# Experts' weights in 2 MB transfers, paired attention heads and a shorter one-hot path in a two-block forward pass

## The chip, the cores and the metric

The kernel runs on one core of a Trainium2 chip. A core has the matmul engine TensorE (PE in the profile, its weight loads are PEld), the element-wise engines VectorE (DVE), ScalarE (ACT) and GpSimd (POOL), SyncE (SP), which here issues nearly all of the large transfers, and 16 DMA engines that move the data between the chip's memory and the core's own. The metric is the device time of one execution in microseconds. A change counts here as faster or slower when it moves the time by more than 2%.

## The reference, cut to what matters

256 tokens of width 1024 pass through two chained blocks, all in float32.

```python
def first_block(x, p, ...):
    h = rms_norm(x, norm_mix)
    z = h @ w_in                                    # u (512), q, k, v (8 heads x 64)
    y_pool = multiscale_pool(u, w_pool, pool_scale)
    y_attn = neighbourhood_attention(q, k, v, q_norm, k_norm, rpb)
    x = x + concatenate([y_pool, y_attn]) @ w_out
    x = x + expert_choice_ffn(rms_norm(x, norm_ffn), w_router, w_gate, w_up, w_down)
    g = sigmoid(rms_norm(x, norm_ple) @ w_ple_gate)
    return x + g * rms_norm(p @ w_ple_proj, norm_ple_post)

def expert_choice_ffn(h, w_router, w_gate, w_up, w_down):      # 16 experts, cap = 32 tokens each
    aff = softmax(h @ w_router)
    gates, idx = top_k(aff.transpose(0, 2, 1), cap)            # every expert takes its 32 best tokens
    xe = h[bidx, idx]
    a, b = xe @ w_gate, xe @ w_up                              # per expert 1024 x 2048 each
    ye = (silu(a) * b) @ w_down                                # per expert 2048 x 1024
    return zeros_like(h).at[bidx, idx].add(ye * gates)
```

The second block (attention over compressed, selected and windowed keys, an mLSTM, attention over a memory, a merge and a dense feed-forward layer) is computed as before and is not touched by the change. The experts' three matrices are 24 MB for each of 16 experts, 384 MB in all, out of about 517 MB that the execution moves.

## The kernel before

**The stages.** The profile's span of 1677.9 us falls into four stretches. Up to about 112 us the first block's mixing runs: the products with `w_in`, the pooling branch, eight attention heads, and `w_out`. From 112 to 165 us come the router, the choice of tokens, the gather of the chosen tokens by one-hot products, and the first expert. From 165 to 1090 us the other experts stream through. From 1090 us on the end of the first block and the second block run.

**The plan and the ring.** Every large weight is an entry of `plan` (built at L251 to L305): `chunk` (L256) loads 256 columns of a matrix, `rows` (L263) whole rows. An expert is 8 entries of `w_gate`, 8 of `w_up` and 8 of `w_down`, of 1 MB each: tile `w` of 128 partitions x 2048 floats. For `w_gate` and `w_up` a partition takes one row of 8 KB, for `w_down` two rows of 4 KB. Four chunks of `w_mem_kv` come ahead of experts 2 to 5, `w_ple_proj` ahead of expert 6, and a chunk of `w_ple_gate` in the middle of the last expert's `w_down`. `issue()` walks the plan in order on SP's queue and takes a slot of a ring for each entry: ring A of 3 slots, B of 7 and C of 6 (`RING_A, RING_B, RING_C`, L28), besides the single places hTl and hT, which `lend()` offers once each when the tile there is no longer needed (hTl after the last `w_in` product, hT after the router's product). `release()` gives a slot back once its products have been issued, and calls `issue()`. Ring C closes after expert 1, so in the stream ten slots are in use. After the experts only ring A goes on.

**The expert's loop.** For each of `w_gate` and `w_up` eight entries are multiplied, four products of 128 x 512 on column groups each (the profile shows pairs of these groups side by side), into tile `z`. Then silu, the product of the two halves (`sa`), four transposes, and eight entries of `w_down` into `s` or `tp`, the scatter by the one-hot `SG`, and the addition to `xs`. For the first expert the gather of the tokens is interleaved with these products.

**The first stage.** Generators run beside the `w_in` products and are pumped by ticks: `na` takes the heads one after the other (`na_scores`: scores, bias, exp; the scaling; `na_pv`: transposes and the product with `v`, which is written for two heads at once). `NA` is the delay in ticks between these steps. A head's scores are two products of 64 x 128 by 64 x 256, on partitions 0 to 63 for the even heads, 64 to 127 for the odd ones.

**The choice of tokens.** Four rounds of max, max_index and match_replace give 32 values (`gt`) and indices (`ix`) per expert. `slot_rows` casts indices to float (`ixf`), spreads them over a block-diagonal tile (`ibd`) and broadcasts it to all partitions with a product by `ones`; `one_hot` compares with the partition's number. The first 24 indices go through POOL, the last 8 through DVE, so there are two products and eight compares. `low_parts(1)` subtracts on POOL in between. Then the gather multiplies the tokens (`wh`, `wl`: high and low parts) by the one-hots.

All compute instructions go through one helper and have line L184 in the profile; transfers of the plan have L256 or L263.

Of the kernel before, what the change touches and what calls it, by code (L numbers as in the profile page):

```python
# [27 lines left out]
RING_A, RING_B, RING_C = 3, 7, 6  # L28
WBUFS, WBUFS2 = 3, 7

LIM, NA, QKT, PLT = 2, 1, 7, 10
# [76 lines left out]
class Clock:  # L108
# [53 lines left out]
    def arrival(self, t):  # L162
        self.dma = max(self.dma, self.last, self.now()) + DMAT
        self.ready[t.tensor.name] = [(0, 2048, self.dma + DMAL)]

    def there(self, t):
        return self.ready[t.tensor.name][0][2]
# [21 lines left out]
def body(ctx, tc, I, out, cst, dbg=None, upto=None):  # L189
# [43 lines left out]
    ra = ctx.enter_context(sbpool("ringA", RING_A))  # L233
    wps = ctx.enter_context(sbpool("wsplit", WBUFS, "right"))
    rb_cm = sbpool("ringB", RING_B, "right")
# [30 lines left out]

    w_in, w_out, w_gate, w_up, w_down = I["w_in"], I["w_out"], I["w_gate"], I["w_up"], I["w_down"]
# [8 lines left out]
    for e in range(NE):  # L276
# [105 lines left out]
    rings = {"A": ra, "B": rb}  # L382
    free = ["A"] * RING_A + ["B"] * RING_B
    open_rings = set("AB")
    RING_TAG = {r: r for r in ("hT", "hTl", "gm0", "ynT", "qT")}

    def issue(limit=10 ** 9):
        while state["issued"] < min(len(plan), limit):
            n = state["issued"]
            c = [i for i, r in enumerate(free) if r in open_rings and (r not in "BC" or n < N_MOE)]  # L390
            if not c:
                return
            r = free.pop(c[0])
            t = T(rings[r], [P, 2048], RING_TAG.get(r, "w"))
            plan[n](t)
            clk.arrival(t)
            tiles[n], pool_of[n] = t, r
            state["issued"] += 1

    def lend(r, n):  # L400

        open_rings.add(r)
        free[:0] = [r] * n
        issue()
        open_rings.discard(r)
# [49 lines left out]
    for r in range(4):  # L455
        nc.sync.dma_start(BB[r % 2 * 64:(r % 2 + 1) * 64, r // 2],
                       src(rpb, (7 - r) * 31 - 48, [[1, 64], [465, 8], [1, 157]]))
    gc = {}
# [312 lines left out]

    table(AF.Exp)
# [50 lines left out]
    def na_scores(h):  # L823
        pr, a = divmod(h, 2)
        b = bias.pop(h)
        s = T(ps, [P, 2, S], "s", 2)
        for tt in range(2):
            pe.matmul(s[:, tt], qT[a * 64:(a + 1) * 64, pr, tt * P:(tt + 1) * P], kT[a * 64:(a + 1) * 64, pr],
                      start=True, stop=True)
        e = T(pt_, [P, 2, S], "e", 2)  # L830
        mx = T(sm, [P, 4], "mx")
        for tt in range(2):
            dve.tensor_tensor_reduce(e[:, tt], s[:, tt], b[:, tt].rearrange("p a b -> p (a b)"), -1.0, BIGF,
                                     OP.add, OP.min, mx[:, tt:tt + 1])
            act.activation(e[:, tt], e[:, tt], AF.Exp, bias=mx[:, tt:tt + 1], scale=-1.0,
                           accum_out=mx[:, 2 + tt:3 + tt])
        if h + 2 < 8:
            na_bias(h + 2)
        yield e, NA
        r = T(sm, [P, 2], "rr")  # L840
        dve.reciprocal(r, mx[:, 2:4])
        for tt in range(2):
            dve.tensor_scalar(e[:, tt], e[:, tt], r[:, tt:tt + 1], None, op0=OP.mult)
        yield e, NA

    ets = {}

    def na_pv(h, e):
        pr, a = divmod(h, 2)
# [6 lines left out]
        yield NA  # L856
        ets[a] = et
        if a == 0:
            return
# [1277 lines left out]
```

## Time and profile before

| | |
|---|---|
| time, median of 3 runs | 1679.8 us |
| the profiled execution's own time | 1679.82 us |
| its span | 1677.9 us |
| PE busy | 1341.8 us (80%) |
| DVE, ACT, POOL busy | 563.7, 398.0, 50.0 us |
| moved by DMA | 516.69 MB |
| mean granted clock of TensorE | 0.838 of full speed |

The page's second part cuts the span into 40 equal slices of about 42 us and gives a digit for each engine's busy share; below them stand the granted clock and the share in which the DMA engines were moving data. The views named further on give the same quantities for any stretch, the instructions of an engine in order of time with what ended the idle time before each, and sums of such idle time by what ended it.

### The profile page before, as it was taken

To read this page: it belongs to the slowest core of one execution; us is meant where nothing else is said; L and a number is where in the kernel's file an instruction comes from. 1 tells how busy PE (TensorE), PEld (TensorE's weight loads), DVE (VectorE), ACT (ScalarE), POOL (GpSimd) and SP (SyncE) were. 2 spreads that over 40 slices of the span, in tenths; PEclk is the share of its full clock that TensorE was granted. 3 is DMA by queue.
4 is the path that set the end of the run, shared out by engine and by line. 5 is a ranking of instruction groups with operands and counts; after the bars stand their busy time and mean duration, and the time that the engine had idled before them with its cause. 6 is when DMAs were issued, how large, how long until landed. Compare 5 with 4: busy or idle time off the path is not lost.

```text
span 1677.9 us, 20652 instructions
## 1 busy us (share of the span) xinstructions
PE 1341.8 (80%) x8442; PEld 776.2 (46%) x8442; DVE 563.7 (34%) x1221; ACT 398.0 (24%) x786; POOL 50.0 (3%) x76
## 2 busy tenths in 40 slices
PE   7978677776776667666666666698999999999998
PEld 7853131221221111011011011198989987999997
DVE  6762111001020001001001010085676766776553
ACT  4541000000010000000000000053556555455441
POOL 1331000000000000000000000000000000000000
PEclk9989876777776776777777677699999999999999
DMA  9568999999999999999999999964544444737550
GB/s 310 224 267 320 415 413 410 417 414 409 418 417 415 417 419 414 416 421 414 415 420 416 415 418 418 385 190 121 157 127 125 128 125 108 232 122 268 176 176 25
DMA packets 175326, 516.69 MB, mean 308 GB/s; under 512 B 11892, under 2 KB 102880, under 8 KB 142464
## 3 DMA queue, kind: packets, MB, share of 16 engines
q1 hardware_dynamic: 173696, 512.04, 79.8%
q0 software_dynamic: 1376, 3.28, 0.5%
q8 instruction: 66, 1.08, 0.3%
q14 instruction: 28, 0.23, 0.0%
q10 hardware_dynamic: 160, 0.07, 0.0%
HBM read 514.30 MB, written 1.05 MB: 307 GB/s over the span
## 4 chain that ended last, share of the span: by engine, by line
DMA 49%; PE 39%; DVE 6%; ACT 3%; issue 1%; SPq 1%; DVEq 0%; ACTq 0%
PE z L184 27%; DMA w<-in_w_up 17%; DMA w<-in_w_down 15%; DMA w<-in_w_gate 14%; PE tp L184 4%; PE dn L184 4%; PE s L184 4%; DMA w<-in_w_mem_kv 2%; DVE wl L184 1%; PE po L184 1%; ACT E L184 1%; DVE rs_t L184 1%; DVE X L184 1%; ACT wh L184 0%; SPq L263 0%
## 5 line engine op out<-in xcount | busy, mean ns | idle before, releaser
L184 PE MATMUL z<-w,xe 128*32 128x512 f32 x2040 | 348.5, 790 | 158.0 <-DMA w<-in_w_up 109.7
L184 DVE TENSOR_TENSOR wl<-w,wh 128x1024 fp32r<-128x1024 f32 (+1 forms) x209 | 224.5, 1098 | 131.3 <-ACT wh L184 130.9
L184 PEld LDWEIGHTS z<-w,xe 128*32 128x32 f32 x2040 | 53.5, 125 | 429.6 <-DMA w<-in_w_up 244.0
L184 ACT ACTIVATE wh<-w 128x1024 fp32r<-128x1024 f32 (+1 forms) x209 | 193.4, 952 | 80.1 <-PE z L184 35.7
L184 DVE TENSOR_TENSOR sa<-sa,z 128x512 f32<-128x512 f32 x15 | 10.3, 687 | 500.9 <-PE z L184 500.9
L184 PE MATMUL tp<-w,ht 128*32 128x512 f32 x512 | 97.4, 864 | 52.2 <-DMA w<-in_w_down 46.7
L184 PE MATMUL z<-wh,hT 128*128 128x256 f32 x448 | 133.7, 298 | 2.2 <-ACT wh L184 1.9
L184 PE MATMUL z<-wl,hT 128*128 128x256 f32 x448 | 127.5, 285 | 1.6 <-DVE wl L184 1.6
L184 PE MATMUL z<-wh,hTl 128*128 128x256 f32 x448 | 127.5, 285 | 0.4 <-DVE hTl L184 0.4
L184 PE MATMUL s<-w,ht 128*32 128x512 f32 x448 | 88.0, 888 | 42.4 <-DMA w<-in_w_down 37.6
L184 PEld LDWEIGHTS z<-wh,hT 128*128 128x128 f32 x448 | 85.7, 191 | 7.9 <-issue 4.8
L184 PEld LDWEIGHTS z<-wl,hT 128*128 128x128 f32 x448 | 86.2, 192 | 2.3 <-DVE wl L184 2.0
L184 PEld LDWEIGHTS z<-wh,hTl 128*128 128x128 f32 x448 | 85.6, 191 | 0.6 <-DVE hTl L184 0.6
L184 ACT ACTIVATE ht<-tp 128x512 f32<-128x512 f32 x15 | 9.0, 597 | 321.9 <-PE tp L184 321.9
L184 PE MATMUL z<-x4Th,wl 128*128 128x256 f32 x288 | 81.4, 283 | 0.0
L184 PE MATMUL z<-x4Th,wh 128*128 128x256 f32 x288 | 81.3, 282 | 0.0
L184 PE MATMUL z<-x4Tl,wh 128*128 128x256 f32 x288 | 81.2, 282 | 0.0
L184 PE MATMUL z<-hT,wh 128*128 128x256 f32 (+1 forms) x264 | 78.2, 296 | 0.0
L184 PE MATMUL z<-hT,wl 128*128 128x256 f32 (+1 forms) x264 | 74.3, 281 | 0.0
L184 PE MATMUL z<-hTl,wh 128*128 128x256 f32 (+1 forms) x264 | 74.0, 280 | 0.0
L184 PEld LDWEIGHTS tp<-w,ht 128*32 128x32 f32 x512 | 13.4, 130 | 125.2 <-DMA w<-in_w_down 112.7
L184 PEld LDWEIGHTS s<-w,ht 128*32 128x32 f32 x448 | 11.7, 131 | 111.1 <-DMA w<-in_w_down 100.9
(480 smaller groups left out, 2029.2 us busy)
## 6 DMA issues: line engine op xcount, KB each, us to landing
w<-in_w_up SPq DMA_DIRECT2D x128, 1024.0 KB, 19.8
w<-in_w_gate SPq DMA_DIRECT2D x127, 1024.0 KB, 19.5
w<-in_w_down SPq DMA_DIRECT2D x127, 1024.0 KB, 20.1
w<-in_w_in SPq DMA_DIRECT2D x35, 1024.0 KB, 5.4
w<-in_w_ffn_in SPq DMA_DIRECT2D x22, 1024.0 KB, 5.2
w<-in_w_ffn_down SPq DMA_DIRECT2D x11, 1024.0 KB, 4.9
w<-in_w_out SPq DMA_DIRECT2D x8, 1024.0 KB, 10.9
w<-in_w_mem_kv SPq DMA_DIRECT2D x4, 1024.0 KB, 19.3
```

What stands on the lines that cost most here:

```text
L184: return f(*a, **k)
```

## The change

- `w_gate`, `w_up` and `w_down` are loaded in pairs of plan entries: one transfer of 2 MB into a tile of 128 x 4096, where each partition takes 16 KB that lie together in memory (two rows of `w_gate` or `w_up`, four of `w_down`). The rings are counted in pairs: A 1, B 4, C 3, the same 16 MB. Other entries take one half of a pair's tile. A pair is issued when both halves of a tile are free. hTl and hT are lent together after the router's product, for the first two `w_down` entries.
- So that rows fit the partitions that they arrive on, the tokens' features are permuted where they are written (`by_rows`), the norm's gain is loaded once more in that order (`GCF`), and silu and the product of the halves write through a permuted view.
- In the second block ring A has two slots, and a single slot D is opened after ring B is closed.
- Heads are handled in pairs: the scores of two heads alternate between partitions 0 to 63 and 64 to 127; the softmax, transposes and products with `v` follow per pair, with `NA` 3.
- The one-hots: one spread of all 32 indices directly from the integers, one product, four compares. Both tokens' low parts are taken ahead of the choice.
- `spin(8)` at the start and `spin(16)` ahead of the choice issue products of a tile of zeros whose result nobody reads.

```diff
-RING_A, RING_B, RING_C = 3, 7, 6
+RING_A, RING_B, RING_C = 1, 4, 3
-LIM, NA, QKT, PLT = 2, 1, 7, 10
+LIM, NA, QKT, PLT = 2, 3, 7, 10
...
+    def pair(w, at):
+        def f(t):
+            nc.sync.dma_start(t, src(w, at, [[4096, P], [1, 4096]]))
+        def one(u):
+            def f(t):
+                nc.sync.dma_start(t, src(w, at + u * 2048, [[4096, P], [1, 2048]]))
+            return f
+        PAIRS[len(plan)] = f
+        plan.extend(one(u) for u in range(2))
...
-        for kt in range(8):
-            rows(w_gate, e * D + kt * P, 1, 2048)
-        for kt in range(8):
-            rows(w_up, e * D + kt * P, 1, 2048)
-        for s in range(8):
-            if e == NE - 1 and s == 4:
+        for w in (w_gate, w_up):
+            for b in range(4):
+                pair(w, (e * D + b * 256) * 2048)
+        for b in range(4):
+            if e == NE - 1 and b == 2:
                 N_PLE = len(plan)
                 chunk(I["w_ple_gate"], 0, width=D)
-            rows(w_down, e * 2048 + s * 256, 2, D)
+            pair(w_down, (e * 2048 + b * 512) * D)
...
     def issue(limit=10 ** 9):
         while state["issued"] < min(len(plan), limit):
             n = state["issued"]
-            c = [i for i, r in enumerate(free) if r in open_rings and (r not in "BC" or n < N_MOE)]
-            if not c:
+            ok = [s for s in free if s[0] in open_rings and (s[0] not in "BC" or n < N_MOE)]
+            alone = [s for s in ok if s[1] is None]
+            if n in PAIRS and len(alone) < 2:
+                whole = [s for s in ok if s[1] is not None and s[2] == 0 and other(s) in ok]
+                if not whole:
+                    return
+                s = whole[0]
+                PAIRS[n](bigs[s[0], s[1]])
+                took(n, slot(s), s)
+                took(n + 1, slot(other(s)), other(s))
+                continue
+            if not ok:
                 return
...
+    def spin(n, tag="z", bufs=2):
+        o = T(ps, [P, S], tag, bufs)
+        for _ in range(n):
+            nc.tensor.matmul(o[:, :P], still, still, start=True, stop=True)
+    still = T(cp, [P, P], "still")
+    dve.memset(still, 0.0)
+    spin(8)
...
+    def na_scores(pr):
+        s = [T(ps, [P, 2, S], "s", 2) for _ in range(2)]
         for tt in range(2):
+            for a in range(2):
+                r = slice(a * 64, (a + 1) * 64)
+                pe.matmul(s[a][:, tt], qT[r, pr, tt * P:(tt + 1) * P], kT[r, pr], start=True, stop=True)
+        return s
...
+        for pr in range(2 * hh, 2 * hh + 3):
+            more = pr < 2 * hh + 2
+            if more:
+                s = na_scores(pr)
             if prev is not None:
+                ets = [na_turn(prev[0])]
+                yield 1
+                ets.append(na_turn(prev[1]))
+            if more:
+                es, mx = na_weights(pr, s)
+            yield 2
+            if more:
+                na_scale(es, mx)
+            if prev is not None:
+                na_values(pr - 1, ets)
+            yield NA
+            prev = es
...
-    lend("hTl", 1)
...
-    lend("hT", 1)
+    lend("hTl", "hT")
...
     for tt in range(2):
+        act.activation(by_rows(xnh[tt], True), by_rows(xs[:, tt]), AF.Copy, scale=rr[:, tt:tt + 1])
         for h in range(2):
             v = slice(h * 512, (h + 1) * 512)
             xn = xw[:, v]
-            act.activation(xn, xs[:, tt, v], AF.Copy, scale=rr[:, tt:tt + 1])
+            act.activation(by_rows(xn, True), by_rows(xs[:, tt, v]), AF.Copy, scale=rr[:, tt:tt + 1])
             pool.tensor_tensor(xnl[tt][:, v], xn, xnh[tt][:, v].bitcast(F32), OP.subtract)
...
+    spin(16)
     for r in range(4):
...
-    early = slot_rows(pool, 0, 24)
-    low_parts(1)
-    late = slot_rows(dve, 24, 8)
+    dve.tensor_tensor(ibd.rearrange("p (e c) -> p e c", c=CAP), ident[:NE, :NE, None].to_broadcast([NE, NE, CAP]),
+                      ix[:, None, :].to_broadcast([NE, NE, CAP]), OP.mult)
+    pib = T(ps, [P, NE * CAP], "s", 2)
+    pe.matmul(pib, ones16, ibd, start=True, stop=True)
     for g in range(2):
-        one_hot(early, 0, 24, g)
-        one_hot(late, 24, 8, g)
+        for tt in range(2):
+            dve.tensor_scalar(oh[g][:, tt], pib.rearrange("p (g e c) -> p g e c", g=2, c=CAP)[:, g],
+                              K("pidx")[:, tt:tt + 1], None, op0=OP.is_equal)
...
-                act.activation(sa, z, AF.Silu)
+                act.activation(sa.rearrange("p (i q) -> p i q", i=4), z.rearrange("p (q i) -> p i q", i=4), AF.Silu)
...
+    room("D", ctx.enter_context(sbpool("ringD", 1, "right")), 1, 1)
```

SP's queue where the ring is first reused, before: tiles `w` are 1 MB slots, hT is the borrowed place, `in_w_up` and `in_w_down` belong to expert 0, `in_w_gate` to expert 1.

```order
L263 DMA w_1278<-in_w_up 128x2048
L263 DMA w_1280<-in_w_down 128x2x1024
L263 DMA hT_1304<-in_w_down 128x2x1024
L263 DMA w_1406<-in_w_down 128x2x1024
L263 DMA w_1423<-in_w_down 128x2x1024
L263 DMA w_1429<-in_w_down 128x2x1024
L263 DMA w_1446<-in_w_down 128x2x1024
L263 DMA w_1452<-in_w_down 128x2x1024
L263 DMA w_1469<-in_w_down 128x2x1024
L263 DMA w_1475<-in_w_gate 128x2048
L263 DMA w_1502<-in_w_gate 128x2048
L263 DMA w_1514<-in_w_gate 128x2048
```

The same place in the changed kernel: wA, wB and wC are pairs of 2 MB in the three rings.

```order
L275 DMA wC_1252<-in_w_up 128x4096
L275 DMA wC_1253<-in_w_up 128x4096
L275 DMA wC_1254<-in_w_up 128x4096
L279 DMA hTl_1280<-in_w_down 128x2048
L279 DMA hT_1282<-in_w_down 128x2048
L275 DMA wB_78<-in_w_down 128x4096
L275 DMA wB_79<-in_w_down 128x4096
L275 DMA wB_80<-in_w_down 128x4096
L275 DMA wB_81<-in_w_gate 128x4096
L275 DMA wA_77<-in_w_gate 128x4096
L275 DMA wB_78<-in_w_gate 128x4096
L275 DMA wB_79<-in_w_gate 128x4096
```

The last two entries of `w_down` in a borrowed place are its first two now, and every later entry of the experts stands as one instruction for two.

DVE's queue at the choice of tokens, before: the last round of max and max_index, then the last eight indices (cast `ixf`, spread `ibd`), the compares into `wh` by parts of 24 and of 8 indices, and the first write of the gathered tokens `xe`.

```order
L184 MAX gt_1351<-affT_1364 16x8
L184 MAX_INDEX ix_1352<-gt_1351,affT_1364 16x8
L184 CAST ixf_1353<-ix_1352 16x8
L184 TENSOR_TENSOR ibd_1354<-CI_76,ixf_1353 16x128
L184 TENSOR_SCALAR wh_1337<-s_1371,C_75 128x8x24 x2
L184 TENSOR_SCALAR wh_1337<-s_1379,C_75 128x8x8 x2
L184 TENSOR_SCALAR xe_1389<-s_286_1391,GC_75_314 128x256
```

In the changed kernel:

```order
L187 MAX gt_1333<-affT_1362 16x8
L187 MAX_INDEX ix_1334<-gt_1333,affT_1362 16x8
L187 TENSOR_TENSOR ibd_1335<-CI_76,ix_1334 16x512
L187 TENSOR_SCALAR wh_1313<-s_1368,C_75 128x256 x4
L187 TENSOR_SCALAR xe_1374<-s_262_1376,GCF_325 128x256
```

The cast is gone from this place (it comes later, with `rep`), the spread is one instruction of 16 x 512, and of the two rows of compares, which stood there twice, one with four instructions is left.

PE's queue at the same place, before: the router's product with `wrg`, two small transposes of maxima and of `aff`, the two broadcasts of `ibd`, and the first product of the gather.

```order
L184 MATMUL s_1295<-hT_1019,wrg_1021 32x256 x8
L184 MATMUL s_1325<-C_75,affT_1323 128x16 x2
L184 MATMUL tp_1346<-CI_76,aff_1331 16x128 x2
L184 MATMUL s_1371<-ibd_1354,ones_200_1022 128x384
L184 MATMUL s_1379<-ibd_1354,ones_200_1022 128x128
L184 MATMUL s_286_1391<-wh_1337,wh_1291 128x256
```

In the changed kernel, where `still` is the tile of zeros:

```order
L187 MATMUL s_1271<-hT_1012,wrg_1014 32x256 x8
L187 MATMUL s_1303<-C_75,affT_1301 128x16 x2
L187 MATMUL tp_1328<-CI_76,aff_1309 16x128 x2
L827 MATMUL z_1336<-still_136 128x128 x16
L187 MATMUL s_1368<-ibd_1335,ones_185_1015 128x512
L187 MATMUL s_262_1376<-wh_1313,wh_1267 128x256
```

Sixteen products of zeros stand between the transposes and the broadcast, which is one product of 512 columns.

## Rows read from the trace of the kernel before

**Rows 1.** The page: busy time, and the DMA engines' share in tenths in 40 slices.

```profile
PE 1341.8 (80%) x8442; PEld 776.2 (46%) x8442; DVE 563.7 (34%) x1221; ACT 398.0 (24%) x786; POOL 50.0 (3%) x76
...
DMA  9568999999999999999999999964544444737550
```

**Rows 2.** Windows: start:end and length, busy time of each engine, clock, DMA, GB/s.

```profile
core 0: us, PE busy (x) PEld busy (x) DVE busy (x) ACT busy (x) POOL busy (x), PEclk, DMA share, GB/s
0.00:112.00 112.00, 101.38 (x628) 86.33 (x628) 73.99 (x197) 53.22 (x98) 34.00 (x51) 1.00 0.75 255
165.00:1090.00 925.00, 637.38 (x3273) 150.15 (x3265) 78.81 (x145) 40.92 (x66) 2.27 (x5) 0.73 1.02 414
1090.00:1678.00 588.00, 563.26 (x4265) 522.13 (x4261) 389.10 (x814) 291.92 (x601) 1.07 (x2) 0.98 0.48 149
```

**Rows 3.** Waits of PE by what ended them, 300 to 1000 us: total, times, longest.

```profile
PE z L184 <- DMA w<-in_w_up: 86.5, 95, 1.6
PE tp L184 <- DMA w<-in_w_down: 34.3, 32, 1.6
```

**Rows 4.** Windows with `w_gate` or `w_up` alone, `w_down` alone, a `w_ple_gate` chunk alone.

```profile
903.00:931.00 28.00, 20.12 (x104) 4.25 (x96) 3.32 (x5) 1.28 (x2) 0.00 (x0) 0.68 1.01 421
882.00:894.00 12.00, 9.23 (x44) 1.81 (x36) 0.95 (x2) 0.60 (x1) 0.00 (x0) 0.60 1.03 410
1089.00:1093.00 4.00, 2.98 (x14) 1.29 (x8) 0.75 (x1) 0.69 (x1) 0.00 (x0) 0.50 1.06 348
```

**Rows 5.** SP's issues in order of time: start, duration, queue, line, what, how many.

```profile
162.22 2.90 SPq L263 DMA_DIRECT2D w<-in_w_gate  x4
...
662.01 17.74 SPq L263 DMA_DIRECT2D w<-in_w_up  x8
...
722.31 17.73 SPq L263 DMA_DIRECT2D w<-in_w_up  x8
```

**Rows 6.** Windows of 2 us around the first expert.

```profile
130.00:132.00 2.00, 1.44 (x10) 0.27 (x9) 0.48 (x1) 0.47 (x1) 0.00 (x0) 0.50 0.00 0
160.00:162.00 2.00, 2.00 (x26) 0.54 (x19) 0.00 (x0) 0.00 (x0) 1.59 (x4) 1.00 0.22 60
164.00:166.00 2.00, 2.00 (x24) 0.52 (x16) 0.00 (x0) 0.00 (x0) 1.15 (x3) 1.00 0.87 360
```

**Rows 7.** PE in order of time: a head's scores, and the products with `v` of two heads.

```profile
38.91 1.13 PE L184 MATMUL s<-kT,qT 64*128 64x256 f32 x4
...
46.56 1.12 PE L184 MATMUL y<-et,vt 128*64 128x256 f32 x8
```

**Rows 8.** PE in order of time, around the choice of tokens and the gather.

```profile
118.49 0.59 PE L184 MATMUL tp<-CI,aff 128*16 128x128 f32 x2 [1.89 <-DVE aff L184]
124.59 0.68 PE L184 MATMUL s<-ibd,ones 16*128 16x384 f32 x1 [5.51 <-POOL ibd L184]
127.37 0.47 PE L184 MATMUL s<-ibd,ones 16*128 16x128 f32 x1 [2.10 <-DVE ibd L184]
128.31 0.77 PE L184 MATMUL s<-wh,wh 128*128 128x256 f32 x2 [0.47 <-DVE wh L184]
```

**Rows 9.** DVE in order of time, then POOL, at the same place.

```profile
124.25 2.76 DVE L184 CAST ixf<-ix 16x8 f32<-16x8 uint32 x1
127.04 0.28 DVE L184 TENSOR_TENSOR ibd<-CI,ixf 16x128 fp32r<-16x128 f32 x1
127.25 2.14 DVE L184 TENSOR_SCALAR wh<-s,C 128x192 fp32r<-128x192 f32 x8
...
123.71 0.82 POOL L184 TENSOR_TENSOR ibd<-CI,ixf 16x384 fp32r<-16x384 f32 x1
124.50 2.48 POOL L184 TENSOR_TENSOR wl<-wl,wh 128x512 fp32r<-128x512 f32 x2
```

**Rows 10.** PE in order of time: the first `w_in` products, and the last expert's last `w_down`.

```profile
12.89 0.41 PE L184 MATMUL z<-wh,hT 128*128 128x256 f32 x1
...
1088.46 1.94 PE L184 MATMUL tp<-w,ht 128*32 128x512 f32 x8 [1.11 <-DMA w<-in_w_down]
```

More of the change, by code (lines that the diff above doesn't have):

```diff
@@ L163, in arrival @@
         self.dma = max(self.dma, self.last, self.now()) + DMAT
-        self.ready[t.tensor.name] = [(0, 2048, self.dma + DMAL)]
+        lo = t.offset % t.ap[0][0]
+        r = self.ready.get(t.tensor.name, [])
+        self.ready[t.tensor.name] = [v for v in r if v[1] < lo or lo + 2047 < v[0]] + [(lo, lo + 2047, self.dma + DMAL)]
     def there(self, t):
-        return self.ready[t.tensor.name][0][2]
+        lo = t.offset % t.ap[0][0]
+        return max(v[2] for v in self.ready[t.tensor.name] if v[0] <= lo + 2047 and lo <= v[1])
     def now(self):
@@ L381, in body, with room, other, slot @@
     state = {"issued": 0, "used": 0}
-    rings = {"A": ra, "B": rb}
-    free = ["A"] * RING_A + ["B"] * RING_B
-    open_rings = set("AB")
+    rings = {}
+    bigs, free, open_rings = {}, [], set()
     RING_TAG = {r: r for r in ("hT", "hTl", "gm0", "ynT", "qT")}
+    def room(r, pl, n, width=2):
+        for i in range(n):
+            bigs[r, i] = T(pl, [P, width * 2048], "w" + r, n)
+            free.extend((r, i, h) for h in range(width))
+        open_rings.add(r)
+    room("A", ra, RING_A)
+    room("B", rb, RING_B)
+    def other(s):
+        return s[0], s[1], 1 - s[2]
+    def slot(s):
+        if s[1] is None:
+            return T(rings[s[0]], [P, 2048], RING_TAG[s[0]])
+        return bigs[s[0], s[1]][:, s[2] * 2048:(s[2] + 1) * 2048]
+    def took(n, t, s):
+        free.remove(s)
+        clk.arrival(t)
+        tiles[n], pool_of[n] = t, s
+        state["issued"] = n + 1
     def issue(limit=10 ** 9):
@@ L389, in issue, with lend @@
             n = state["issued"]
-            c = [i for i, r in enumerate(free) if r in open_rings and (r not in "BC" or n < N_MOE)]
-            if not c:
+            ok = [s for s in free if s[0] in open_rings and (s[0] not in "BC" or n < N_MOE)]
[10 more added lines that the diff above has]
+            if not ok:
                 return
-            r = free.pop(c[0])
-            t = T(rings[r], [P, 2048], RING_TAG.get(r, "w"))
+            halves = [s for s in ok if s[1] is not None and other(s) not in ok]
+            s = (alone + halves + ok)[0]
+            t = slot(s)
             plan[n](t)
[L396 to L403, printed above, removed]
+            took(n, t, s)
+    def lend(*rs):
+        open_rings.update(rs)
+        free[:0] = [(r, None, None) for r in rs]
         issue()
-        open_rings.discard(r)
+        open_rings.difference_update(rs)
     def get():
@@ L846, in body, with na_weights @@
[L846 to L849 removed]
+            for a in range(2):
+                r = slice(a * 64, (a + 1) * 64)
+                pe.matmul(s[a][:, tt], qT[r, pr, tt * P:(tt + 1) * P], kT[r, pr], start=True, stop=True)
+        return s
+    def na_weights(pr, s):
+        es, mx = [], T(sm, [P, 2, 2, 2], "mx")
+        for a in range(2):
+            e = T(pt_, [P, 2, S], "e", 2)
+            b = bias.pop(2 * pr + a)
+            for tt in range(2):
+                dve.tensor_tensor_reduce(e[:, tt], s[a][:, tt], b[:, tt].rearrange("p a b -> p (a b)"), -1.0, BIGF,
+                                         OP.add, OP.min, mx[:, 0, a, tt:tt + 1])
+                act.activation(e[:, tt], e[:, tt], AF.Exp, bias=mx[:, 0, a, tt:tt + 1], scale=-1.0,
+                               accum_out=mx[:, 1, a, tt:tt + 1])
+            if 2 * pr + a + 2 < 8:
+                na_bias(2 * pr + a + 2)
+            es.append(e)
+        return es, mx
@@ L850, in na_pv, with na_scale, na_turn @@
+    def na_scale(es, mx):
+        r = T(sm, [P, 2, 2], "rr")
+        dve.reciprocal(r, mx[:, 1])
+        for a in range(2):
+            for tt in range(2):
+                dve.tensor_scalar(es[a][:, tt], es[a][:, tt], r[:, a, tt:tt + 1], None, op0=OP.mult)
+    def na_turn(e):
         pt = T(ps, [P, 2, S], "tp", TPB[0])
@@ L920, in body @@
                 GCs[name] = GC1
+            g = T(ps, [P, P], "tp", TPB[0])
+            for i in range(2):
+                pe.transpose(g[:, 4 * i:4 * i + 4], GRF[:, i::2], ident[:4, :4])
+            GCF = T(cp, [P, 8], "GCF")
+            dve.tensor_copy(GCF, g[:, :8])
         if n == 3:
```

82 lines of the change are left out of this document (21 added, 61 removed).

## The prediction

> **What bounds the kernel now.** I began with the page. TensorE is busy 80% of the span, but in the row under it the DMA engines are at 9 tenths in 22 slices together and at 3 to 7 tenths behind [rows 1]. So there are stages with different limits, and the second view, the windows, separates them [rows 2]. From 165 to 1090 us the DMA share is 1.02 and 414 GB/s flow while TensorE is busy 637 of 925 us: transfers set the pace. Before that, from 0 to 112 us, and behind it, from 1090 us on, TensorE is busy 101 of 112 and 563 of 588 us: products set the pace, and a transfer gained there is worth nothing. The third view, TensorE's waits in the stream, agrees: for `w_up` alone it waited 95 times and 86.5 us, each wait at most 1.6 us [rows 3]. The start of the stream counts as much as its rate, since whatever the first block gains is only worth something if it lets transfers begin sooner.
>
> **1. The rate of the stream.** Fourth view, windows in which only one kind of transfer is in flight: runs of 8 KB (`w_gate`, `w_up`) go at 421 GB/s, of 4 KB (`w_down`) at 410, of 1 KB at 348 [rows 4]. For one of 16 engines that is 8192 B x 16 / 421 = 311.3 ns for a run of 8 KB, 159.8 ns for 4 KB. The second 4 KB cost 151.5 ns, so some 8.3 ns are paid per run whatever its length. (The 1 KB row gives 47.1 ns, which is the same line within 1 ns.) A run of 16 KB by this line takes 311.3 + 2 x 151.5 = 614.3 ns, which is 426.7 GB/s. An expert now takes 722.31 - 662.01 = 60.30 us from one `w_up` to the next [rows 5], and its bytes by rows 4 give the same: 16.78 MB / 421 + 8.39 MB / 410 = 60.31 us. Then: 25.17 MB / 426.7 = 58.97 us, or 1.33 us less per expert.
>
> How many experts get this? The transfers stand still for want of a slot twice: at 130 to 132 us nothing flows, and at 160 to 162 us it is 60 GB/s; by 164 us it flows again, after the issues at 162.22 us [rows 5, 6]. The bytes moved until then (18 MB of places, hT and hTl included, and 10 slots reissued: 28 MB) are waited for by products, not the other way round, and they are the same 28 MB in the changed kernel. So the rate counts for the other 356 MB, 14.83 experts: **-19.7 us**.
>
> Bounds: if a 16 KB run goes no faster than one of 8 KB, an expert takes 59.78 us and the gain is 7.8 us (only `w_down` improves). If the constant share vanished altogether, 4096 B in 151.5 ns on 16 engines are 432.6 GB/s, 58.17 us and -31.5 us. I take the line, since three lengths lie on it.
>
> The page "SBUF — State Buffer" of the Trainium skill (The DMA setup-cost knee) fits a transfer by 2 us and its bytes at 436 GB/s, and advises the largest single transfers; twelve fewer transfers per expert would by that save 24 us of each. The trace disagrees: in rows 4 one transfer of 1 MB follows the other at 421 GB/s, 2.49 us each, with nothing of a fixed cost left between them. By that rule the sum would be some 356 us larger; by the row the number of transfers is worth nothing, and only the length of a run counts.
>
> **2. The start of the stream.** After 28 MB the next free place before is the slot whose products end at about 162.2 us [rows 5]. A pair needs one more entry's products, about 0.9 us by 8 products at full clock (half of the 1.94 at half clock [rows 10]): **+0.9**. Against it stands what the first block gains:
>
> - Zero products at the start. An early `w_in` product of 256 columns shows 0.41 us with its pipeline's end [rows 10], at a clock that has not risen yet. If it rises sooner, some of the next are quicker, but at this point they wait for splits too; between 0 and -2.5 us (a dozen products at 0.2 us less), taken -0.5.
> - Scores in pairs. One head's two products hold TensorE for 1.06 us (from 38.91, 1.13 with the pipeline's end). The product with `v`, four products on alternating halves, moves double the work in 1.12 us [rows 7]. So halves run side by side, and two heads take about 1.06 rather than 2.12 us: 4 x 1.06 = 4.2 us. Paired steps stand closer to the softmax that they wait for, so between +1 and -4.2 us, taken -3.2.
> - One-hots. Now the gather begins at 128.31, after the cast that took 2.76 us beside POOL's 2.48 us subtraction, the spread, the small product and four compares [rows 8, 9]. Then: from 124.25 the spread of 512 (0.28 for 128 elements, 0.82 for 384 on POOL: 0.7), one product (0.68 for 384 columns: 0.8), two compares (2.14 / 8 to 2.14 / 4: 0.9 together), so 126.7, 1.6 us sooner. But the 16 zero products stand ahead of it on TensorE. One of 128 columns takes a quarter of a head's scores, 0.27 us, or 0.54 at half clock; from 119.1 that ends between 123.4 and 127.7, where 125 would be needed. So between -1.6 and +1.1 us, taken -0.8.
> - The clock. At 130 to 132 us it is 0.50 and TensorE busy 1.44 of 2.00 us; it is 1.00 behind 134 [rows 6]. If zero products bring it to full before the gather, about 5 us of products at half speed take half: between 0 and -2.8, taken -2.5.
>
> Together -7.0 + 0.9 = **-6.1 us**, from +2 to -10. Nothing in between takes it back, since the stream begins with that release.
>
> **3. What pairs cost.** After the last bytes TensorE has twice the products to do: where 8 took 1.94 us at half clock [rows 10], 16 stand now, so +1.0 us at full and **+1.9 us** at half clock, which I take since that row's clock is half. A place comes back in pairs, so the first half of each waits about one transfer (2.49 us) longer than before. Ten slots are 24.9 us of transfers at 2.49 us; of these one pair is being multiplied and one is landing, which leaves some 15 us queued. Only where the memory chunks with products of their own (ahead of experts 2 to 5) hold TensorE for longer could the queue run empty: 0 to 2 us in all, taken **+1**. The permuted silu, writes and gains lie beside transfers and cost nothing; without that cover the last expert alone would show some 0.6 us. The later second block issues its chunks in almost the same order, with products ahead of transfers by rows 2: 0, +-1.
>
> **Sum**: -19.7 - 6.1 + 1.9 + 1.0 = -22.9 us on the profiled execution's 1679.82 us (the median of the runs is 1679.8): 1656.9, which I round to **1657 us**, -1.4%.
>
> **The rivals.**
>
> *A 16 KB run is no better than one of 8 KB* (it could be cut into pieces of at most 8 KB). For it: no row shows a longer run. Against: three points on one line. -7.8 - 6.1 + 2.9 = -11: 1669 us. Chance 0.20.
>
> *The constant share vanishes.* -31.5 - 6.1 + 2.9 = -34.7: 1645 us, at the border of 2% (1646). For it: half as many transfers and a quarter to a half as many runs, if part of the cost is one of transfers. Against: the same line. Chance 0.08. The page "DMA: Bandwidth & Descriptors" (Where 436 GB/s comes from) gives 435.2 GB/s as the ceiling of the ports, which by estimate is 1640 us; 426.7 lies below it, and no window of rows 4 reaches it.
>
> *Slower: longer runs at a wider pitch are read at less.* A partition's run now starts 16 KB after its neighbour's, instead of 8. If this lost as much as going back to `w_down`'s 410 GB/s, an expert takes 61.38 us: +16.0 - 6.1 + 2.9 = +12.8, 1693 us. It decides from a period above 60.5 us (416 GB/s), and beyond 2% from 62.8 us (401 GB/s). Against: going from a pitch of 4 to 8 KB brought 410 to 421. Chance 0.07. The second page (Latency and other measured facts) reports a loss of rate for row pitches at large powers of two, from 512 KB on, which speaks in this direction; no run here shows it.
>
> *The stream runs dry.* Five pairs are too few, and a gap of about 1 us comes with each expert (the product of the halves, its transposes and the scatter stand between transfers): +14.8 - 19.7 - 6.1 + 2.9 = -8, 1672 us. Against: the 15 us that are queued by part 3. Chance 0.05. The remaining 0.60 is the forecast.
>
> **The numbers.** The forecast's own range, by the start's +2 to -10 and the line's error, is 1651 to 1663 us. With the first rival, and a part of the others, 1646 to 1674 holds 0.8. Less than 2% is about what a comparison of this kernel can tell from no change. Faster by more (below 1646): half of the second rival and a little of the rest, 0.07. Slower by more (above 1713): 0.04. Else 0.89.
>
> **What would show it.** Windows of the changed stream: 427 GB/s in `w_gate` as in `w_down`, and 59.0 us from one expert to the next; 421 and 59.8 for the first rival, 410 or less for the third. Start: the gather near 124 rather than 128.31, at clock 1.00, and full flow from about 158 instead of 164. Scores: two heads in 1.1 us. The end of the last `w_down` products some 2 us after its last bytes' old place. It would be wrong if the second block moved by more than 2 us, or if transfers stood still after 165 us.

## The result, and the profile after

| | before | after |
|---|---|---|
| time, median | 1679.76 us (4 runs) | 1655.68 us (1652.59 to 1658.83, 4 runs) |
| ratio after / before | | 0.986, interval 0.984 to 0.988 |
| profiled execution, its span | 1679.82, 1677.9 us | 1652.59, 1650.7 us |

One of the four executions of the kernel before took 3156.62 us, and the ratio leaves it out. The forecast was 1657 us. The change is 24 us faster, less than 2%. In a second job the same kernel gave 1655.17 us, ratio 0.985 [0.983, 0.988]. The sum came out; two of its terms did not, and they nearly cancel, as the trace shows.

The page of the changed kernel, busy time and the DMA row, then its windows with the columns of [rows 2]:

```profile
PE 1278.3 (77%) x8491; PEld 782.6 (47%) x8491; DVE 562.8 (34%) x1214; ACT 397.0 (24%) x786; POOL 49.2 (3%) x75
...
DMA  9559999999999999999999999965534445737550
```

```profile
0.00:112.00 112.00, 95.99 (x624) 82.88 (x625) 73.54 (x191) 50.63 (x95) 34.22 (x52) 0.94 0.68 221
165.00:1070.00 905.00, 583.53 (x3277) 162.83 (x3266) 79.26 (x145) 40.81 (x66) 4.09 (x8) 0.78 1.01 424
1070.00:1650.00 580.00, 551.86 (x4265) 511.32 (x4261) 388.27 (x814) 291.66 (x601) 1.07 (x2) 0.99 0.49 151
420.00:1030.00 610.00, 382.76 (x2154) 93.42 (x2156) 49.08 (x87) 24.12 (x40) 0.00 (x0) 0.78 1.01 426
```

The stream runs at 424 GB/s where it ran at 414 [rows 2]. The row from 420 to 1030 us, inside the stream, serves below to compare kernels; the kernel before has 417 GB/s there:

```profile
420.00:1030.00 610.00, 413.81 (x2095) 83.39 (x2097) 48.80 (x87) 23.43 (x38) 0.00 (x0) 0.72 1.02 417
```

But the first stage moves 221 GB/s rather than 255, and its mean clock fell from 1.00 to 0.94: something waits there that did not before.

TensorE of the changed kernel in order of time, first the place at fault, then the scores, the choice of tokens, and the end of the last expert:

```profile
18.81 0.23 PE L187 MATMUL tp<-CI,GR 14*128 14x14 f32 x1
26.28 0.40 PE L187 MATMUL tp<-CI,plm 4*128 4x4 f32 x2 [7.24 <-DVE GC L187]
...
43.49 1.13 PE L187 MATMUL s<-kT,qT 64*128 64x256 f32 x8
...
122.55 0.58 PE L187 MATMUL tp<-CI,aff 128*16 128x128 f32 x2 [1.89 <-DVE aff L187]
122.93 6.30 PE L827 MATMUL z<-still 128*128 128x128 f32 x32
129.46 0.46 PE L187 MATMUL s<-ibd,ones 16*128 16x512 f32 x1 [0.23 <-DVE ibd L187]
130.60 0.75 PE L187 MATMUL s<-wh,wh 128*128 128x256 f32 x2 [0.67 <-DVE wh L187]
...
1068.13 1.92 PE L187 MATMUL tp<-wB,ht 128*32 128x512 f32 x16 [1.68 <-DMA wB<-in_w_down]
1070.86 0.38 PE L187 MATMUL s<-SG,yh 64*128 64x256 f32 x1 [0.81 <-ACT yh L187]
```

VectorE at the place at fault, from the start of q's normalisation to the copy of the gains, and the same copy in the kernel before:

```profile
19.55 0.69 DVE L187 TENSOR_REDUCE qv<-sq 128x8 f32<-128x512 f32 x1 [0.22 <-ACT sq L187]
...
25.46 0.69 DVE L187 TENSOR_TENSOR qn<-z,rs_y 128x512 f32<-128x512 f32 x1 [0.53 <-DVE rs_y L187]
26.07 0.16 DVE L187 COPY GC<-tp 128x14 f32<-128x14 f32 x1
```

```profile
26.11 0.16 DVE L184 COPY GC<-tp 128x14 f32<-128x14 f32 x1
```

The two transposes of the new gains (`plm`) take the tile `tp`, of which there is one at this point. It is free only when VectorE has copied the gains before them (`GC`), and this copy stands in VectorE's queue behind the whole normalisation of q. The copy is no later than before; what is new is that TensorE waits for it. TensorE stood still for 7.24 us in front of two products of 0.2 us; the k products that filled this time before stand behind them in its queue, and the first of them starts at 26.61 us. The clock fell too: windows of the changed kernel show 0 us busy, then a clock of 0.50, the level of 1.2 GHz. Before, TensorE was busy throughout at 1.00, as the third row shows for the first window:

```profile
22.00:26.00 4.00, 0.00 (x0) 0.00 (x0) 3.16 (x11) 0.96 (x1) 1.30 (x2) 0.56 1.09 348
28.00:32.00 4.00, 4.00 (x21) 4.00 (x20) 0.02 (x1) 0.00 (x0) 0.00 (x0) 0.50 1.09 346
```

```profile
22.00:26.00 4.00, 4.00 (x34) 3.82 (x32) 3.46 (x16) 1.46 (x2) 0.75 (x1) 1.00 1.10 349
```

From trace to trace the 27.2 us between the two spans are made up like this. By 165 us 45.49 MB had landed, before 45.83 MB: the stream is 0.8 us later, not 6 us earlier. The last expert's last `w_down` products begin at 1068.13 us, before at 1088.46 [rows 10]: 20.3 us earlier. From them to the first scatter it is 2.73 us, before 2.75. And from there to the end of the span it is 579.8 us, before 586.7: **6.9 us less in a stage that the change was not expected to move**. The first scatter before:

```profile
1091.21 0.58 PE L184 MATMUL s<-SG,yh 64*128 64x256 f32 x1 [0.81 <-ACT yh L184]
```

So the open questions were the wait at the start, the cause of the higher rate, and the second block.

### The profile page after: what moved, and what is told of

Same layout as the page of the kernel before. It is cut to its first block, busy times and chain, and to the rows that moved or that the text cites. A ratio compares the mean times of both kernels' runs of the same rounds, so it can differ in the third digit from the quotient of the medians.

```text
span 1650.7 us, 20362 instructions
## 1 busy us (share of the span) xinstructions
PE 1278.3 (77%) x8491; PEld 782.6 (47%) x8491; DVE 562.8 (34%) x1214; ACT 397.0 (24%) x786; POOL 49.2 (3%) x75
## 4 chain that ended last, share of the span: by engine, by line
PE 44%; DMA 41%; DVE 9%; ACT 5%; issue 2%; DVEq 0%; ACTq 0%
PE z L187 28%; DMA wB<-in_w_down 13%; DMA wB<-in_w_up 12%; DMA wA<-in_w_down 5%; PE tp L187 5%; PE s L187 5%; DMA wB<-in_w_gate 4%; PE dn L187 4%; DMA wA<-in_w_up 4%; DMA wA<-in_w_gate 3%; DVE wl L187 2%; ACT wh L187 1%; ACT E L187 1%; DVE rs_t L187 1%; DVE xs L187 1%
## 5 line engine op out<-in xcount | busy, mean ns | idle before, releaser
L187 PE MATMUL z<-wB,xe 128*32 128x512 f32 x1600 | 246.2, 750 | 141.0 <-DMA wB<-in_w_up 107.2
L187 PEld LDWEIGHTS z<-wB,xe 128*32 128x32 f32 x1600 | 50.8, 125 | 325.2 <-issue 139.7
L187 DVE TENSOR_TENSOR wl<-wA,wh 128x1024 fp32r<-128x1024 f32 (+2 forms) x127 | 139.6, 1120 | 67.5 <-ACT wh L187 67.2
L187 ACT ACTIVATE wh<-wA 128x1024 fp32r<-128x1024 f32 (+2 forms) x127 | 120.1, 969 | 42.3 <-PE z L187 17.5
L187 PE MATMUL tp<-wB,ht 128*32 128x512 f32 x400 | 70.0, 835 | 43.5 <-DMA wB<-in_w_down 40.7
L187 PE MATMUL s<-wB,ht 128*32 128x512 f32 x368 | 64.1, 831 | 42.5 <-DMA wB<-in_w_down 41.1
L187 PE MATMUL z<-wA,xe 128*32 128x512 f32 x400 | 65.9, 789 | 37.7 <-DMA wA<-in_w_up 26.8
L187 DVE TENSOR_TENSOR wl<-wD,wh 128x1024 fp32r<-128x1024 f32 (+1 forms) x64 | 63.7, 1021 | 42.4 <-ACT wh L187 42.4
```

The lines of the kernel that those rows point to most:

```text
L187: return f(*a, **k)
```

## The experiments

Each kernel was timed beside the kernel before on the same chip; ratios are to that.

**The changed kernel again.**

> The changed kernel once more, as the base for the others on this chip and for the spread of its time (1652.6 to 1658.8 us in four runs). Theory A (the second block's 6.9 us less in the first profile are the pace of that execution, not the change): a new profile shows another pace there, between 580 and 587 us from the last scatter to the end, and the time lies at 1652 to 1659. Theory B (they come from the change): 580 us again, within 1 us.

1655.17 us, ratio 0.985 [0.983, 0.988]. From the first scatter (1072.19) to the end it is 581.4 us, between the two theories but 5.3 us under the kernel before: the larger part of the gain in the second block stays. Its products follow one another as fast as in the first trace (116.5 ns, by the measure given with b1), so theory A's other pace did not show.

**The gains' transposes in one tile (e1).**

```diff
-            GC1 = gain_cols(GR1, n1, "GC1", ps)
...
             g = T(ps, [P, P], "tp", TPB[0])
+            pe.transpose(g[:, :n1], GR1[:n1, :], ident[:n1, :n1])
             for i in range(2):
-                pe.transpose(g[:, 4 * i:4 * i + 4], GRF[:, i::2], ident[:4, :4])
+                pe.transpose(g[:, 32 + 4 * i:36 + 4 * i], GRF[:, i::2], ident[:4, :4])
+            GC1 = T(cp, [P, n1], "GC1")
+            dve.tensor_copy(GC1, g[:, :n1])
```

> The two small transposes of the gains go into the same PSUM tile as the gains' transpose before them, instead of a new one. Theory A: what made the first scores 7.2 us later (43.49 instead of 36.24 us) is TensorE's wait for VectorE's copy of that tile; without it the first scores begin near 35 us, the gather near 122 instead of 130.6, and since the stream starts with the release by the first expert's products, the whole is 6 us shorter than the changed kernel. Rival: the stream's start is bound by the transfers of the first 28 MB; then the scores come sooner too, but the whole moves by less than 2 us.

1650.54 us, ratio 0.983 [0.982, 0.985], 4.6 us less than the changed kernel in the same job. TensorE of e1:

```profile
18.70 0.23 PE L187 MATMUL tp<-CI,GR 14*128 14x14 f32 x1
18.78 0.37 PE L187 MATMUL tp<-CI,plm 4*128 4x4 f32 x2
...
37.37 1.14 PE L187 MATMUL s<-kT,qT 64*128 64x256 f32 x8
...
124.47 0.75 PE L187 MATMUL s<-wh,wh 128*128 128x256 f32 x2 [0.67 <-DVE wh L187]
...
1062.45 3.60 PE L187 MATMUL tp<-wB,ht 128*32 128x512 f32 x16 [3.03 <-DMA wB<-in_w_down]
```

The wait is gone, scores and gather come 6.1 us sooner, and at 300 us 104.8 MB have landed instead of 102.1, which is 6.3 us at 427 GB/s. The last products begin 5.7 us sooner (1062.45). So theory A holds and the rival falls. By the times alone it would be close, since the intervals of the two ratios overlap; the trace decides it, and four more kernels built on e1 below have medians of 1648 to 1652 us. In this execution 1.7 us are lost again at the very end, where the last sixteen products ran at half clock, 3.60 us instead of 1.92.

**Two runs of 8 KB in one transfer of 2 MB (e2), and in two of 1 MB (e3).**

```diff
-            nc.sync.dma_start(t, src(w, at, [[4096, P], [1, 4096]]))
e2:
+            nc.sync.dma_start(t.rearrange("p (i n) -> p i n", i=2), src(w, at, [[2048, P], [2048 * P, 2], [1, 2048]]))
e3:
+            for u in range(2):
+                nc.sync.dma_start(t[:, u * 2048:(u + 1) * 2048], src(w, at + u * 2048, [[4096, P], [1, 2048]]))
```

> Still one transfer of 2 MB per pair, but each partition takes two runs of 8 KB that lie 1 MB apart, instead of one of 16 KB (the weights' rows then meet other features, so what is computed is not the reference's). Theory A (only the length of a run counts): 421 GB/s, 59.8 us per expert, 12 us slower than the changed kernel. Rival (half as many transfers are what helped): 427 GB/s and 59.0 us, no change.

> Each pair in two transfers of 1 MB, each with a run of 8 KB from every partition's 16 KB. Theory A (only the length of a run counts): as with two runs in one transfer, 421 GB/s, 59.8 us per expert, 12 us slower than the changed kernel. Rival 1 (the number of transfers counts too): slower than that by more than 3 us. Rival 2 (a pitch of 16 KB between partitions slows reading): below 421 GB/s.

1669.2 us (ratio 0.994 [0.992, 0.995]) and 1666.7 us (0.992 [0.991, 0.994]): 14 and 12 us more than the changed kernel. The same window of both, e2 first:

```profile
420.00:1030.00 610.00, 382.77 (x2115) 92.36 (x2117) 49.43 (x87) 23.45 (x38) 0.00 (x0) 0.78 1.01 420
```

```profile
420.00:1030.00 610.00, 412.28 (x2123) 79.66 (x2121) 49.02 (x87) 23.43 (x38) 0.00 (x0) 0.73 1.01 420
```

Both have 420 GB/s, with half as many transfers or as many as before, with neighbours 8 KB or 16 KB apart. So the number of transfers gives nothing, the pitch costs nothing, and the whole difference to 426 is the run.

**Runs of 16 KB in two transfers of 1 MB: the lower and the upper 64 partitions (e4), even and odd ones (e8).**

```diff
-            nc.sync.dma_start(t, src(w, at, [[4096, P], [1, 4096]]))
+            for u in range(2):
e4:
+                nc.sync.dma_start(t[u * 64:u * 64 + 64], src(w, at + u * 64 * 4096, [[4096, 64], [1, 4096]]))
e8:
+                nc.sync.dma_start(t[u::2], src(w, at + u * 4096, [[8192, 64], [1, 4096]]))
```

> From the changed kernel: each pair in two transfers of 1 MB, each for 64 partitions with one run of 16 KB from each. Theory A (only the length of a run counts): 427 GB/s and 59.0 us per expert as in the changed kernel, though the number of transfers is that of before; the whole within 2 us of it. Rival (it was the smaller number of transfers, or that each feeds all partitions): 421 GB/s or less, 12 us or more slower.

> From the changed kernel: each pair in two transfers of 1 MB, one for the even and one for the odd partitions, with a run of 16 KB for each. It keeps runs of 16 KB and has as many transfers as before, but unlike the version with the lower and the upper 64 partitions it spreads each transfer over all of them. Theory A (only the length of a run counts, and the lower or upper half alone is slow since it reaches half of the ways into the memory on the core): 427 GB/s, within 2 us of the changed kernel. Rival (fewer partitions per transfer are slow as such): 218 GB/s as there.

e4 took 2393 us (2244 to 2567, a spread that stays open): theory A failed, by far. e8 took 1659.1 us, ratio 0.987 [0.985, 0.989]. The windows, e4 first:

```profile
420.00:1030.00 610.00, 271.80 (x1152) 78.10 (x1152) 27.37 (x52) 15.22 (x25) 0.00 (x0) 0.61 1.01 218
```

```profile
420.00:1030.00 610.00, 391.45 (x2143) 100.71 (x2145) 49.06 (x87) 23.43 (x38) 0.00 (x0) 0.76 1.00 425
```

In both the DMA engines are busy all the time; in e4 they move half. So it is not the 64 partitions but which: every other one reaches 425, a block of 64 gets 218. The page "SBUF — State Buffer" of the Trainium skill (Door 1: The DMA port swizzle) says that partitions 0 to 63 lie behind 8 of 16 ports and gives 218 GB/s as their limit; the trace agrees, with 218 for the two halves in turn. e8 confirms what e2 and e3 showed: with 16 KB runs, 1 MB transfers flow as 2 MB ones do. It is still 4 us slower than the changed kernel, more than the 2 us expected. Its trace is short of 1.1 MB, 2.5 us, by 420 us already: the clock was 0.54 from 130 to 134 us, and the issue that restarts the transfers stands at 165.64 us, 2.2 us later (e5 below shows what that clock is worth). Between 420 and 1030 us it is short of another 0.8 MB, 2 us, whose cause stays open.

**Without products of zeros (e5).** From e1, `spin(8)` and `spin(16)` left out.

> From the version with both gains' transposes in one tile (e1): the products of zeros are left out at both places. Theory A (they buy clock): the first w_in products at half clock as before, the scores some 1.5 us later, the clock at half from the gather on for some 5 us, the stream's start 3 to 4 us later; the whole 3 to 4 us longer than e1. Rival (they only fill idle time): within 1 us of e1, or faster, if they hold up the broadcast.

1651.5 us, ratio 0.983 [0.982, 0.985]: as e1, within what can be told. The window of e1 at the gather, then that of e5:

```profile
124.00:128.00 4.00, 2.92 (x20) 1.75 (x21) 1.98 (x5) 0.47 (x1) 0.00 (x0) 1.00 0.95 403
```

```profile
124.00:128.00 4.00, 3.43 (x16) 2.03 (x16) 1.52 (x4) 0.47 (x1) 0.00 (x0) 0.50 0.98 414
```

Without zeros the gather began no later (124.00 us) but ran at half clock, and the issue that restarts the transfers, first in e1, then in e5, stands 1.9 us later:

```profile
157.28 2.04 SPq L275 DMA_DIRECT2D wB<-in_w_gate  x2
```

```profile
159.22 2.04 SPq L275 DMA_DIRECT2D wB<-in_w_gate  x2
```

From the gather to this issue it is 32.8 us in e1 and 35.2 in e5, so the full clock is worth 2.4 us here. But the zeros do not secure it. In the second trace of the changed kernel, with all sixteen, TensorE was busy for 2.0 of the 4 us before 130 us, the clock at the gather was 0.50, and the same stretch took 35.2 us too (129.59 to 164.83):

```profile
126.00:130.00 4.00, 1.99 (x14) 1.44 (x12) 3.28 (x8) 0.11 (x1) 1.77 (x2) 0.90 0.96 412
130.00:134.00 4.00, 3.44 (x16) 1.72 (x15) 1.10 (x3) 0.47 (x1) 0.00 (x0) 0.50 1.01 422
```

The eight zeros at the start gave nothing: the scores began at 36.74 us without them, and at 36.92 to 37.37 in e1, e6 and e7, which have them. So the sixteen are worth about 2 us in those executions in which the clock stays up, too little to be seen in the whole, and the eight none.

**Heads not alternating (e6).** From e1, the two loops of `na_scores` exchanged.

> From e1: the four score products of a pair of heads in the order head 1, head 1, head 2, head 2 rather than alternating. Theory A (products on partitions 0 to 63 and 64 to 127 run side by side): only the middle two overlap, so a pair takes 1.6 us of TensorE rather than 1.06, four times 0.53 = 2.1 us; the router 2 us later and the whole 2 us longer. Rival (they do not run side by side; the shorter time has another cause): no change.

1648.3 us, ratio 0.981 [0.979, 0.983]: not slower. The trace has the pair's products in 1.14 us, as e1 has:

```profile
36.92 1.14 PE L187 MATMUL s<-kT,qT 64*128 64x256 f32 x8
```

They start in twos, 0.02 us apart, though both products of one head stand ahead of the other's in the queue; one head's alone, in the kernel before, start 0.2 to 0.3 us apart. So the halves do run side by side, but it is enough that the four products stand together; the alternation gives nothing. My theory A, by which only the middle two would overlap, was wrong.

**The kernel before with zeros alone (b1).** `spin(16)` ahead of the choice, with its tile.

> The kernel before with only sixteen products of zeros ahead of the choice of tokens. Theory A: they end near 125 us, at most 0.8 us after the broadcast could begin; the clock is full at the gather, which gives 2 us; the whole 1 to 2 us shorter than before. Theory B (rival): they delay the broadcast by as much as the clock gives back, no change. From its trace also: if the second block's products of 256 columns follow one another in 118.4 ns, as in the first trace of the kernel before, that pace belongs to the kernel; if in 116.5 ns, to the execution or the chip, and most of the second block's 6.9 us are not the change's.

1680.5 us, ratio 1.000 [0.999, 1.001]: no change. That is theory B's time, but not its reason. The zeros put off only the first broadcast, by 0.6 us (6.70 us behind the router's transposes instead of 6.10 [rows 8]); the gather stands 9.83 us behind them, as before (9.82). What they bought was gone by then: TensorE was busy for 0.27 of the 2 us from 126, and at the gather, from 130 to 134 us, the clock was 0.50 again:

```profile
126.00:128.00 2.00, 0.27 (x1) 0.18 (x1) 1.97 (x4) 0.00 (x0) 1.33 (x2) 1.00 1.03 420
130.00:134.00 4.00, 3.44 (x16) 1.48 (x15) 0.48 (x1) 0.47 (x1) 0.00 (x0) 0.50 0.01 2
```

Its second block has 586.6 us, with 118.3 ns from one product to the next (mean distance of starts, of those 100 to 130 ns apart, in the last 560 us), the same as before, while all traces of the changed kernel and its variants so far have 116.3 to 116.6. The pace therefore belongs to the kernel, not to the execution.

**32 bytes of padding, in the kernel before (p1) and in e1 (p2).**

```diff
     C = T(cp, [P, _LATE0 - P], "C")
+    T(cp, [P, 8], "pad")
```

> The kernel before with one unused tile of 32 bytes per partition among the constants, so that the tiles allocated behind it (the tokens' hT, hTl, the halves wh and wl of the second block) start 32 bytes later; nothing else. Theory A (the place of the operands sets the pace of the products: 118.4 ns from one 256-column product to the next in both traces with the places of before, 116.5 ns in all with those of the changed kernel, which are 32 bytes further by the same measure): 116.5 ns, the second block 581 to 582 us instead of 586.6, the whole 5 to 7 us shorter, 1674 us. Rival (the pace has another cause in the changed kernel): 118.4 ns, 586.6 us, no change.

> The same unused 32 bytes in e1, which put hT and its like back on a multiple of 64 bytes. Theory A: 118.4 ns, the second block 586 to 587 us, the whole 5 to 7 us longer than e1. Rival: 116.5 ns, no change.

p1: 1676.2 us, ratio 0.9975 [0.996, 0.999]. One unused tile of 32 bytes makes the kernel before 3.6 us faster. Its pace is 116.3 ns, and from the first scatter to the end it is 581.7 us, 5.0 less. A group of products from 1200 to 1600 us in the kernel before, then in p1 (busy, mean ns of one with its pipeline's end):

```profile
L184 PE MATMUL z<-wh,hTl 128*128 128x256 f32 x320 | 90.4, 282 | 0.4 <-DVE hTl L184 0.4
```

```profile
L184 PE MATMUL z<-wh,hTl 128*128 128x256 f32 x320 | 89.6, 280 | 0.4 <-DVE hTl L184 0.4
```

p2 did not slow e1 down: 1649.2 us, 0.983 [0.981, 0.985], a pace of 117.0 ns, and 580.0 us in the second block. But the mean hides that one sort of products did slow down. Of each pair of names the first is the operand that is streamed and the second the one loaded as weights. Products that stream hTl, from 1090 to 1640 us, in e1, then in p2:

```profile
L187 PE MATMUL z<-hTl,wh 128*128 128x256 f32 x224 | 62.3, 278 | 0.0
```

```profile
L187 PE MATMUL z<-hTl,wh 128*128 128x256 f32 x224 | 62.9, 281 | 0.0
```

Those that stream hT or hTl follow one another in 115.4 ns in e1 and p1, and in 118.2 in p2 as in the kernel before. Those with hT or hTl as weights take 117.9 in e1, 117.3 in p1 and 117.5 in p2, and 119.7 in the kernel before. In the built programs hT and hTl start on a multiple of 128 bytes in the kernel before and in b1, 32 bytes past one in the changed kernel, e1 and p1, and 64 past one in p2. So theory A is right that the place of the operands sets the pace. Its rule, a start on a multiple of 64 bytes, holds in these runs for hT and hTl as they are streamed; as weights only the place on a multiple of 128 was slow. Three places make no general rule, and why they differ stays open. The slower products of p2 add up to 1.8 us, which the whole does not show: with the same pace the second block took 579 to 584 us in the traces of the changed kernel and its variants.

**Zeros ahead of the last products (e7).** From e1:

```diff
+            if e == NE - 1 and s == 6:
+                spin(8)
             w = get().rearrange("p (k n) -> p k n", k=2)
```

> From e1: eight products of zeros ahead of the last expert's last pair of w_down, where TensorE waits 1.7 to 3.0 us for the transfer. The last sixteen products took 1.92 us in some traces and 3.6 in others, by the granted clock there. Theory A: with the zeros the clock is full, 1.92 us every time, and the whole is 0 to 1.7 us shorter than e1, with less spread. Rival: they end after the transfer has landed and delay it, or the clock stays at half; no change or up to 1 us longer.

1647.9 us, ratio 0.982 [0.980, 0.983], lower than e1's 0.983 but with overlapping intervals. TensorE of e7:

```profile
1057.02 1.92 PE L187 MATMUL tp<-wB,ht 128*32 128x512 f32 x16 [1.21 <-DMA wB<-in_w_down]
1058.87 2.05 PE L827 MATMUL z<-still 128*128 128x128 f32 x16
1062.00 1.92 PE L187 MATMUL tp<-wB,ht 128*32 128x512 f32 x16 [1.08 <-DMA wB<-in_w_down]
```

The zeros end before the transfer lands, and the last products run at full clock. That is what theory A says for one execution; that it does so in each is not shown, and five traces without these zeros have 1.92 us as well (both of the changed kernel, e5, e6 and p2). With e6 it is among the two fastest versions, 6 to 7 us under the changed kernel by the ratios.

## Why the prediction was right, step by step

- **What bounds the kernel**: right. The stream's rate carried most of the gain.
- **The rate, -19.7 us**: right, and for the stated reason. 426.7 GB/s were forecast, 426 to 428 came. An expert takes 58.8 us by the waits for its first `w_up` (675.48, 734.28, 793.10 us), forecast 58.97. That is a little more than was asked of it: with the +1 for an empty queue in it, the stretch from 165 us to the last products gave 21.1 us, where 18.7 were forecast. e2, e3 and e8 show that the run's length alone does it, as the straight line through [rows 4] said. The rule of a fixed cost per transfer was rightly set aside: half as many transfers gave nothing in e2.
- **The start, -6.1 us**: failed, it came out at +0.8. The step that failed is the sentence "The permuted silu, writes and gains lie beside transfers and cost nothing". It put the two new transposes of the gains at nothing, and did not ask which tile they write, who must release it and what stands behind them on TensorE. In the changed kernel the gather stands at 130.60 us at full clock, where the sign asked for was near 124. The other parts of the term were well sized: scores to router's transposes 79.06 us instead of 82.25, -3.2 as forecast; from those transposes to the gather 8.05 instead of 9.82, so -1.8, just past the better end of its range; from the gather to the reissue that restarts the transfers 32.8 us (163.40) instead of 33.9 (162.22). By e5, which has pairs at half clock and 35.2 us there, the last is +1.3 for the pair (+0.9 forecast) and -2.4 for the clock (-2.5), and the second trace of the changed kernel lacks the latter. Together they made up for most of the wait's 7.2 us. Without it, in e1, that reissue stands at 157.28 us, 4.9 us ahead of before, where 6.1 were forecast; the difference is that e1's scores begin at 37.37 us, 1.1 us behind before, though the zeros at the start had been taken as -0.5.
- **Pairs**: +1.9 at the end did not come in the profiled run (1.92 us at full clock for twice the products, 1.94 at half before), and did in e1's (3.60). Both ends of that bound exist, and which one comes is the clock's level there: of the seven traces with pairs of 2 MB and no zeros at the end, five had 1.92 us, e1 and e2 more than 3. The prediction took the rarer case. The +1 for an empty queue cannot be told apart from the stream's own gain.
- **The second block, 0 +-1**: failed; it is 5 to 7 us shorter, and a move of more than 2 us there was one of the prediction's own signs of being wrong. The mechanism is none of those listed: TensorE's products go 1.6% faster since their operands start at another address, a side effect of 32 bytes that the new gains take among the constants. p1 shows it in the kernel before, where the same 32 bytes give 5.0 us of that stage, and the changed kernel's operands lie as p1's do. The step that failed is "in almost the same order, with products ahead of transfers": instructions and queues were counted for that stage, and equal instructions taken for equal time.
- **Rivals**: the first (no better than 8 KB) is excluded by e2 against the changed kernel, the third by 426 GB/s at a pitch of 16 KB, the fourth by a DMA share of 1.01. The second would have shown 432.6 GB/s; the windows of the stream have 426 to 427.

So the time was hit because a missed loss of 7 us and a missed gain of 5 to 7 us lay on either side of a correct main term. That is luck: without the missed wait e1 gave 1650.5 us, just outside the forecast's own range of 1651 to 1663.

## What to carry to other kernels

When a stream is bound by its transfers, fit the time of a run against its length from windows with one kind of transfer each; what a longer run gives is on that line, and the number of transfers is not. An instruction added to a full queue costs what it waits for, not what it takes: ask for every new tile who frees it, and where that stands in the other queue. And before explaining a change in a stage that should not have moved, compare the pace of identical instructions in it; if that differs, pad the allocation in the old kernel and look again.

## What the runs showed of the hardware that was not expected

- Transfers to the lower and the upper 64 partitions in turn ran at 218 GB/s (e4), to every other partition at 425 (e8).
- Products of 256 columns followed one another in 118.3 or 116.3 ns at the same granted clock; 32 bytes in front of their operands turned the one into the other, and gave 3.6 us of the whole (p1). With hT and hTl 64 bytes past a multiple of 128 the products that stream them were slow and those that have them as weights were not (p2).
- Products of two heads on different halves of the partitions start within 0.02 us of each other even when two of one head precede the other's in the queue (e6).
- At the gather the clock was 1.00 in one execution of the changed kernel and 0.50 in another, with the same zeros ahead of it; the difference is 2.4 us.
- One integer spread of 16 x 512 read directly by VectorE takes the place of the cast that had taken 2.76 us [rows 9]: from the end of the last index search to the broadcast it is 1.2 us, before 3.2.
